# Pairs of sequences as units of the sample group's sparse attention, with scores on eight TensorE tiles of 64 rows and 32 columns

## The chip, the cores and the metric

The kernel is one launch on one core of a Trainium2 chip. The metric is the device time of the launch in microseconds (us), as the median of several runs. Four compute engines matter here: TensorE (PE, matmuls and transposes), VectorE (DVE), ScalarE (ACT) and GpSimd (POOL); SyncE's queue (SP) issues the page loads. TensorE writes its results into PSUM, which is handed out in banks of 128 partitions by 512 floats.

## The reference, cut to what matters

Two token groups go through a two-layer decoder trunk: a prompt of 512 tokens, and a sample group of 8 sequences with 8 new tokens each and 4096 past tokens. The change lies in layer 1's sparse attention of the sample group. For every query head it has three branches: compressed keys (255 of them), the past's 64 blocks of 64 keys of which a top-16 choice is kept by a mask, and a window of 512 keys; the new tokens' own 8 keys are added to the last two.

```
s_c = where(ok_c, einsum('btghd,bngd->btghn', qf, kc), NEG);  p_c = softmax(s_c);  o_c = p_c @ vc
imp = einsum('btghn,ns->btgs', p_c, m_ov);  top_v, top_i = top_k(imp, 16)
s_s = where(ok_s, qf . k_sel, NEG);  p_s = softmax(s_s);  o_s = p_s @ v_sel
s_w = where(ok_w, qf . k_win, NEG);  p_w = softmax(s_w);  o_w = p_w @ v_win
return gates[0] * o_c + gates[1] * o_s + gates[2] * o_w
```

A sequence has 16 heads in 4 groups of 4; a group shares its keys and values, and a head is 64 wide. So for one sequence and one group there are 32 query rows (4 heads by 8 tokens), and the scores of a group contract over 64 elements.

## The kernel before

The trunk runs in stages: layer 0, its feed-forward with the compression of the past's pages beside it, the projections of layer 1's attention, the attention itself, the output projection, memory attention and the last feed-forward. The attention stage is the one that matters here. In it two Python generators are woven: `prompt_attend` (40 steps of the prompt's attention, `one`) and `sample_attend` (`other`). The weaving is the loop at the end of `mixer_nsa`: after prompt step `i` it takes sample units until their count is 1.76 (i + 1). The sample generator has 76 units: 4 of compressed scores (two sequences each), 8 windows (one sequence each), and 64 selected units (one sequence, one chunk of 512 past keys). The instructions are then ordered for each engine by a scheduler that works with priorities and modelled times, so what stands next to what on an engine is not in the source; each engine works its own list in order. `together` asks that a group of matmuls follow their first.

One selected unit loads a "page" tile of 1 MB (`pg`, four transfers of 256 KB by `load_pages`, L1106: keys in the first half of a row, values in the second), and then:

- two score matmuls (L1622) into one PSUM bank `ss_ps`. The page's keys lie with one key group in partitions 0 to 63 and the next in 64 to 127; the queries `qz` are stored with zeros in the half that is not theirs, so that each matmul contracts over all 128 rows and gives 64 columns of the array (two groups by 32 rows). The two matmuls write partitions 0 to 63 and 64 to 127.
- the mask, the scale and the row's maximum on DVE (`scores`, L1480), which empties the bank, and the exponential with its sum on ACT (`expo`, L1483);
- four transposes (L1492) into `st_ps`, a copy to `spT` on ACT or DVE in turn (L1494), and 16 matmuls of 32 columns (L1499) into `oa_ps`, a bank that collects all 8 chunks of a sequence.

After a sequence's eighth chunk, L1631 to L1644 weigh the chunks and add them to `orow`; at the end of all, `or_ps` (L1662) transposes `orow` into `oT`, which the output projection reads. The scores of the prompt (`sc_ps`), the compressed keys (`cs_ps`), the windows (`sw_ps`) and the new keys (`sn_ps`) share three PSUM banks (tag "sc") with `ss_ps`; transposes and small outputs share three more (tag "tp"). Pages have five buffers at first; whenever ten prompt steps are done, the queries of a prompt group are no longer needed and give one buffer more (`pgq`).

Of the kernel before, what the change touches and what calls it, by code (L numbers as in the profile page):

```python
# [83 lines left out]
_nv("nmask", 512)  # L84
# [8 lines left out]
def _nsa_constants():  # L93
# [11 lines left out]
    bb, t = j // 64, p % TS  # L105
    kb, kt = (j % 64) // TS, j % TS
    put("nmask", np.where((bb == kb)[None, :] & (kt[None, :] <= t[:, None]), 0, NEG))
# [54 lines left out]
def tile_step(ctx: ExitStack, tc: tile.TileContext, I, O):  # L162
# [949 lines left out]
    gD = dp.tile([48, TS, NB], F32, name="gD")  # L1112
# [4 lines left out]
    def mixer_nsa():  # L1117
        with ExitStack() as c0:
# [12 lines left out]

            kp = c0.enter_context(pool(name="nkeep", bufs=1))
            qz = kp.tile([P, NB, 2, 64], F32, name="qz")
            G.memset(qz, 0.0)
            ksn = kp.tile([P, 2, 2, 64], F32, name="ksn")
            vsn = kp.tile([64, 512], F32, name="vsn")
            sgate = kp.tile([P, 3, NB], F32, name="sgate")
# [34 lines left out]
            with ExitStack() as c1:  # L1172
# [81 lines left out]
    def nsa_queries(ch, xh, xl, rc, wk, pst, ax, qH, qz):  # L1254
        if True:
            ps = proj_tm(pst, I["w_in1t"][2 + ch], xh, xl, TOKS)
            for i, t0, n, kt in head_rows(ps, rc, wk, late["nrow"][:, 0:64], lambda i: wk.tile([P, 512], F32, tag="kt", name="qt", bufs=5)):
# [12 lines left out]
                else:  # L1270
# [4 lines left out]
                    for e in range(2):  # L1275
                        for b in range(NB):
                            V.tensor_copy(qz[e * 64 : (e + 1) * 64, b, ch, e * 32 : (e + 1) * 32].rearrange("p (h t) -> p h t", h=4),
                                          tp[e * 64 : (e + 1) * 64, 4 * e : 4 * e + 4, b * TS : (b + 1) * TS])

    def nsa_gates(xh, xl, rb, wk, pst, ax, gT, sgate):  # L1280
# [6 lines left out]
        sgt = wk.tile([48, TS, NB], F32, tag="cpg", name="sgt", bufs=1)  # L1287
        V.tensor_scalar_add(sgt, sg[:, TP:].rearrange("p (b t) -> p t b", t=TS), 1.0)
        V.reciprocal(sgt, sgt)
        nc.scalar.dma_start(gD, sgt)  # L1290
        for r in range(3):
            nc.scalar.dma_start(sgate[:, r, :], gD.rearrange("(h r) t b -> r h t b", r=3)[r])
# [71 lines left out]
    def prompt_compressed(N, wk, pa, qH, kc2, gT, pcT):  # L1364
# [21 lines left out]
        for tt, (sc, mx) in enumerate(rows):  # L1386
            V.tensor_reduce(mx, sc, axis=AX.X, op=ALU.add)
            V.reciprocal(mx, mx)
            V.tensor_mul(mx, mx, gT[:, tt, 0::3])
# [8 lines left out]
    def prompt_attend(N, wk, pa, po, qH, ktm, vsb, gT, pcT, vcz, oT):  # L1398
# [3 lines left out]
        for g in range(4):  # L1402
# [11 lines left out]
            for pr in range(2):  # L1414
# [3 lines left out]
                for pieces in (((0, 3),), ((0, 0), (0, 2)), ((0, 1), (1, 1)), ((1, 0), (1, 2)), ((1, 3),)):  # L1418
# [23 lines left out]
                    for i, (br, tt, q) in enumerate(at):  # L1442
                        r = 3 * (4 * g + h0) + 1 + br
                        V.tensor_mul(sm[:, i, :], sm[:, i, :], gT[:, tt, r : r + 4 : 3])
# [29 lines left out]
    def sample_attend(N, wk, page, pa, po, qz, ksn, vsn, sgate, orow, mrow, oT):  # L1474

        def scores(ps, mask, s, mn):
# [6 lines left out]
        def output(o, s, v, first, last, flip, behind=None):  # L1485

            tp = pa.tile([P, 4, P], F32, tag="tp", name="st_ps")
            pT = wk.tile([P, 4, P], F32, tag="spT", name="spT")
            lead = None
            for i in range(4):  # L1490
                with together(lead):
                    mm = TE.transpose(tp[:, i, :], s[:, i * P : (i + 1) * P], ident)  # L1492
                lead = lead or mm.ins
            (S.copy if flip else V.tensor_copy)(pT, tp)  # L1494
            lead = None
            for i in range(4):
                for g in range(4):
                    with together(lead) if lead is not None or behind is None else tc.issue_after(behind):
                        mm = TE.matmul(o[g * 32 : (g + 1) * 32, :], pT[:, i, g * 32 : (g + 1) * 32], v[:, i, g * 64 : (g + 1) * 64],  # L1499
                                       start=first and i == 0, stop=last and i == 3)  # L1500
                    lead = lead or mm.ins
            return mm.ins

        def output_new(o, br, s, first):
# [4 lines left out]
            for g in range(4):  # L1509
                TE.matmul(o[g * 32 : (g + 1) * 32, :], pT[:, g * 32 : (g + 1) * 32], vsn[:, br * 256 + g * 64 : br * 256 + (g + 1) * 64],  # L1510
# [7 lines left out]
        def compressed(b0):  # L1518

            kv = page().rearrange("p (b e i f) -> p b e i f", b=2, e=2, i=2)  # L1520
            for b in range(2):
                nc.sync.dma_start(kv[:, b, 0], kcD[b0 + b])
                nc.sync.dma_start(kv[:, b, 1], vcD[b0 + b])
            ps = pa.tile([P, 2, 256], F32, tag="sc", name="cs_ps")
            for b in range(2):
                for gp in range(2):
                    TE.matmul(ps[gp * 64 : (gp + 1) * 64, b, :], qz[:, b0 + b, gp, :], kv[:, b, 0, gp, :], start=True, stop=True)
            mx = wk.tile([P, 2], F32, tag="cmx", name="cmx")
            V.tensor_reduce(mx, ps[:, :, :255], axis=AX.X, op=ALU.max)
            V.tensor_scalar_mul(mx, mx, -0.125)  # L1530
            p = wk.tile([P, 2, 256], F32, tag="ss", name="cp", bufs=3)
            sm = wk.tile([P, 2], F32, tag="csm", name="csm")
            V.memset(p[:, :, 255:], 0.0)
            for b in range(2):
                S.activation(p[:, b, :255], ps[:, b, :255], AF.Exp, bias=mx[:, b : b + 1], scale=0.125, accum_out=sm[:, b : b + 1])
# [3 lines left out]
            for b in range(2):  # L1539
                for i in range(2):  # L1540
                    TE.transpose(tp[:, b, i, :], p[:, b, i * P : (i + 1) * P], ident)
# [3 lines left out]
            for b in range(2):  # L1545
                for i in range(2):
                    for g in range(4):
                        TE.matmul(oc[g * 32 : (g + 1) * 32, b, :], pT[:, b, i, g * 32 : (g + 1) * 32], kv[:, b, 1, i, g * 64 : (g + 1) * 64],
                                  start=i == 0, stop=i == 1)
            V.tensor_mul(orow[:, b0 : b0 + 2, :], oc, sgate[:, 0, b0 : b0 + 2].unsqueeze(2).to_broadcast([P, 2, 64]))  # L1550
# [5 lines left out]
            q0 = (b0 % 4) * 32  # L1556
            for b in range(2):
# [302 lines left out]
```

## Time and profile before

| what | value |
|---|---|
| time, median of 3 runs (lowest to highest) | 2393.67 us (2391.99 to 2395.39) |
| profiled execution: its time, its span | 2394.9 us, 2393.1 us |
| TensorE busy, share of the span | 2335.8 us, 98% |
| attention stage, about | from 1450 to 1795 us |
| in it, busy: PE, DVE, ACT | 328.4, 263.8, 200.1 us of 345 |

Matmuls are shown with partitions contracted by columns of the array ("128\*64"). A float32 matmul leaves two records, a transpose one. The records of a run of matmuls overlap, so what a run takes is read from its start to the start of the next run, not from the length of a record. The profiled execution lies 1.2 us above the median.

### The profile page before, as it was taken

How to read it: one execution, taken by the hardware profiler on the slowest of the kernel's cores; microseconds unless marked ns; L12 is line 12 of the kernel's file. 1: busy time of each engine (PE TensorE's matmuls, PEld its weight loads, DVE VectorE, ACT ScalarE, POOL GpSimd, SP SyncE). 2: the span in 40 equal slices, each digit the busy share in tenths (PEclk: the TensorE clock that was granted, in tenths of full speed). 3: DMA queues.
4: the chain of work that ended last, by engine and by line, in shares of the span. 5: the costliest groups of instructions: out<-in, count | busy, mean ns of one | idle time of the engine just before them, and what ended most of it. 6: DMA issues, size and time to landing. Idle time of an engine off the chain costs nothing. (4 is left out here: it accounts for less than half of the span.)

```text
span 2393.1 us, 51279 instructions
## 1 busy us (share of the span) xinstructions
PE 2335.8 (98%) x19363; PEld 2118.5 (89%) x19363; DVE 1490.1 (62%) x3357; ACT 1007.3 (42%) x1940; POOL 468.0 (20%) x579
## 2 busy tenths in 40 slices
PE   8999999998999999999999998999999899999999
PEld 8999889986999999999998875566669699999999
DVE  7766564676767777775435867787776774333333
ACT  4333123354555555553224545565564452122221
POOL 2146453121112122213011420000002111010100
PEclk9999999999999999999999999999999999999999
DMA  4221332245366776673421226678872422424222
GB/s 159 80 66 36 132 124 81 76 150 194 112 206 206 212 226 212 201 228 101 135 71 40 87 70 227 215 242 266 265 263 95 166 89 76 161 73 158 72 94 84
DMA packets 181833, 344.25 MB, mean 144 GB/s; under 512 B 21073, under 2 KB 93394, under 8 KB 180050
## 3 DMA queue, kind: packets, MB, share of 16 engines
q1 hardware_dynamic: 173106, 315.75, 41.2%
q10 hardware_dynamic: 8480, 25.23, 2.8%
q8 instruction: 153, 2.51, 0.4%
q14 instruction: 94, 0.77, 0.1%
HBM read 319.44 MB, written 25.47 MB: 144 GB/s over the span
## 5 line engine op out<-in xcount | busy, mean ns | idle before, releaser
L213 ACT CAST whi<-raw 128x1024 fp32r<-128x1024 f32 (+4 forms) x278 | 258.7, 931 | 672.2 <-PE pj L240 568.1
L215 DVE TENSOR_TENSOR wlo<-raw,whi 128x1024 fp32r<-128x1024 f32 (+4 forms) x278 | 317.1, 1141 | 66.5 <-ACT whi L213 58.8
L240 PE MATMUL pj<-fxl,whi 128*128 128x256 f32 (+1 forms) x1408 | 306.8, 296 | 0.0
L240 PE MATMUL pj<-fxh,whi 128*128 128x256 f32 (+1 forms) x1408 | 306.7, 297 | 0.0
L240 PE MATMUL pj<-fxh,wlo 128*128 128x256 f32 (+1 forms) x1408 | 306.2, 296 | 0.0
L1067 DVE TENSOR_TENSOR clo<-craw,chi 128x512 fp32r<-128x512 f32 x256 | 201.6, 802 | 92.2 <-ACT chi L1066 84.1
L240 PEld LDWEIGHTS pj<-fxl,whi 128*128 128x128 f32 x1408 | 237.9, 190 | 0.0
L240 PEld LDWEIGHTS pj<-fxh,wlo 128*128 128x128 f32 x1408 | 237.7, 190 | 0.0
L240 PEld LDWEIGHTS pj<-fxh,whi 128*128 128x128 f32 x1408 | 237.6, 190 | 0.0
L1066 ACT CAST chi<-craw 128x512 fp32r<-128x512 f32 x256 | 155.4, 620 | 117.0 <-PE c_ps L1077 101.0
L967 POOL TENSOR_TENSOR fg<-fg,rb 128x576 f32<-128x576 f32 x44 | 75.7, 1720 | 504.3 <-ACT fg L966 504.1
L240 PE MATMUL pj<-xl,whi 128*128 128x256 f32 (+1 forms) x768 | 171.2, 301 | 0.0
L240 PE MATMUL pj<-xh,wlo 128*128 128x256 f32 (+1 forms) x768 | 169.4, 300 | 0.0
L240 PE MATMUL pj<-xh,whi 128*128 128x256 f32 (+1 forms) x768 | 169.3, 300 | 0.0
L240 PE MATMUL pj<-al,whi 128*128 128x256 f32 x704 | 154.4, 296 | 0.0
L240 PE MATMUL pj<-ah,whi 128*128 128x256 f32 x704 | 154.4, 296 | 0.0
L240 PE MATMUL pj<-ah,wlo 128*128 128x256 f32 x704 | 153.6, 296 | 0.0
L1075 PE MATMUL c_ps<-chi,w1h 128*128 128x256 f32 (+1 forms) x512 | 143.5, 283 | 2.5 <-ACT chi L1066 2.5
L1076 PE MATMUL c_ps<-clo,w1h 128*128 128x256 f32 (+1 forms) x512 | 144.6, 284 | 0.5 <-DVE clo L1067 0.4
L1077 PE MATMUL c_ps<-chi,w1l 128*128 128x256 f32 (+1 forms) x512 | 144.4, 284 | 0.0
L240 PEld LDWEIGHTS pj<-xl,whi 128*128 128x128 f32 x768 | 129.8, 190 | 4.7 <-issue 4.0
L240 PEld LDWEIGHTS pj<-xh,wlo 128*128 128x128 f32 x768 | 129.8, 190 | 2.4 <-issue 1.7
(544 smaller groups left out, 5244.3 us busy)
## 6 DMA issues: line engine op xcount, KB each, us to landing
craw<-in_cmpP SPq DMA_DIRECT2D x512, 128.0 KB, 3.0
pg<-in_slcP SPq DMA_DIRECT2D x192, 256.0 KB, 3.9
raw<-in_w_in SPq DMA_DIRECT2D x48, 512.0 KB, 3.5
raw<-in_w_gate SPq DMA_DIRECT2D x44, 512.0 KB, 3.4
raw<-in_w_up SPq DMA_DIRECT2D x44, 512.0 KB, 3.2
pgq<-in_slcP SPq DMA_DIRECT2D x64, 256.0 KB, 3.9
raw<-in_w_down SPq DMA_DIRECT2D x32, 384.0 KB, 3.7
raw<-in_w_down SPq DMA_DIRECT2D x32, 320.0 KB, 2.9
```

Of the source, the lines that this page charges most:

```text
L213: S.copy(hi, raw)
L215: V.tensor_sub(lo, raw, hi)
L240: TE.matmul(ps[h], w[:, k, :], x[k0 + k][:, t0:t1], start=f and first, stop=e and last)
L967: G.tensor_mul(t, t, rb)
L1066: S.copy(hx, rv)
L1067: V.tensor_sub(lx, rv, hx)
L1075: TE.matmul(ps[:, :n], w1h[:, kv, jj, :], hv, start=jj == 0, stop=False)
L1076: TE.matmul(ps[:, :n], w1h[:, kv, jj, :], lv, start=False, stop=False)
L1077: TE.matmul(ps[:, :n], w1l[:, kv, jj, :], hv, start=False, stop=jj == 7)
```

## The change

The sample's unit becomes a pair of sequences (`pr`, sequences 2 pr and 2 pr + 1), with 40 units in all: 4 compressed, 4 windows and 32 selected. `qz` loses its zeros and is half as wide. The scores of a pair are eight matmuls (`products`), each over 64 rows of the array and 32 of its columns: the row half `x` is the half of the partitions in which the key group lies, the column place is given by group pair and sequence. The four with `x` = 1 fill one bank, the four with `x` = 0 another. Transposes and outputs are then also done for both banks at a time (8 transposes, 32 output matmuls); one bank is copied by ACT and one by DVE. `oa_ps` holds four chunks of a pair instead of eight of a sequence, so after the fourth chunk ACT copies it away. The weaving takes 0.93 units a prompt step. The order of the gates, masks and `orow` follows the new rows; the gates come through two stores and one load.

```diff
-                    while n < 1.76 * (i + 1):
+                    while n < 0.93 * (i + 1):
...
+        SLOTS = [(gp, b) for gp in range(2) for b in range(2)]
+        def products(ps, pr, keys):
+            first = None
+            for b in (1, 0):
+                for x in (1, 0):
+                    for gp in range(2):
+                        i = 2 * gp + b
+                        h = slice(x * 64, (x + 1) * 64)
+                        with together(first):
+                            mm = TE.matmul(ps[x][i * 32 : (i + 1) * 32], qz[h, 2 * pr + b, gp, :], keys(b, gp)[h], start=True, stop=True)
+                        first = first or mm.ins
...
+        def turned(s):
+            tp = [pa.tile([P, 4, P], F32, tag="tp", name="st_ps") for _ in range(2)]
+            pT = [wk.tile([P, 4, P], F32, tag="spT", name="spT") for _ in range(2)]
...
+            S.copy(pT[0], tp[0])
+            V.tensor_copy(pT[1], tp[1])
...
+        def selected(pr):
...
-                pg = page().rearrange("p (k f) -> p k f", k=4)
-                load_pages(b, 4 * c, 4, [lambda k: pg[:, k, :]], I["slcP"])
-                ps = pa.tile([P, 4, P], F32, tag="sc", name="ss_ps")
-                for gp in range(2):
-                    TE.matmul(ps[gp * 64 : (gp + 1) * 64, :, :], qz[:, b, gp, :], pg[:, :, gp * P : (gp + 1) * P], start=True, stop=True)
-                s = wk.tile([P, 512], F32, tag="ss", name="ss", bufs=3)
...
+                pg = []
+                for b in range(2):
+                    p = page().rearrange("p (k f) -> p k f", k=4)
+                    load_pages(2 * pr + b, 4 * c, 4, [lambda k, p=p: p[:, k, :]], I["slcP"])
+                    pg.append(p)
+                ps = [pa.tile([P, 4, P], F32, tag="sc", name="ss_ps") for _ in range(2)]
+                products(ps, pr, lambda b, gp: pg[b][:, :, gp * P : (gp + 1) * P])
+                s = [wk.tile([P, 512], F32, tag="ss", name="ss", bufs=4) for _ in range(2)]
+                for x in range(2):
+                    scores(ps[x].rearrange("p i (k x) -> p (i k) x", k=2),
+                           mrow[:, 2 * pr + x, c * 8 : (c + 1) * 8].unsqueeze(2).to_broadcast([P, 8, 64]),
+                           s[x].rearrange("p (k x) -> p k x", k=8), mn[:, x, c : c + 1])
+                    expo(s[x], mn[:, x, c : c + 1], sm[:, x, c : c + 1])
+                pT = turned(s)
+                if c % 4 == 0:
+                    oa = po.tile([P, 2, 4, 64], F32, tag="oa", name="oa_ps")
+                last = output(lambda x: oa[:, x, c % 4, :], pT, lambda b: pg[b][:, :, 256:], True, last)
+                if c == 3:
+                    S.copy(t, oa)
...
+            for src, dst, c0 in ((t, o1, 0), (oa, o2, 4)):
+                u = wk.tile([P, 2, 4, 64], F32, tag="ss", name="su", bufs=4)
+                for x in range(2):
+                    V.tensor_mul(u[:, x], src[:, x], f[:, x, c0 : c0 + 4].unsqueeze(2).to_broadcast([P, 4, 64]))
+                    V.tensor_reduce(dst[:, x, :], u[:, x].rearrange("p c d -> p d c"), axis=AX.X, op=ALU.add)
```

On TensorE, where the prompt turns to its second group of heads, a selected unit's two score matmuls stand in the kernel before as one row (`sc_ps` and `kt_ps` are the prompt's scores and key transposes):

```order
L1430 MATMUL sc_ps<-kHH,qH 128x512 x2
L1622 MATMUL ss_ps<-pg,qz 64x512 x2
L1430 MATMUL sc_ps<-kLL,qH 128x512 x2
L1412 MATMUL kt_ps<-cst,kd 128x128 x4
L1622 MATMUL ss_ps<-pg,qz 64x512 x2
```

In the changed kernel the eight of a pair stand there in two halves of four, the first four being those with `x` = 1 (one bank), the last four those with `x` = 0:

```order
L1433 MATMUL sc_ps<-kHH,qH 128x512 x2
L1464 MATMUL o_ps<-pcT,vcz 64x512 x2
L1492 MATMUL ss_ps<-pg,qz 32x512 x2
L1492 MATMUL ss_ps<-pgq,qz 32x512 x2
L1433 MATMUL sc_ps<-kLL,qH 128x512 x2
L1415 MATMUL kt_ps<-cst,kd 128x128 x4
L1492 MATMUL ss_ps<-pg,qz 32x512 x2
L1492 MATMUL ss_ps<-pgq,qz 32x512 x2
```

What moved: the prompt's second score matmuls and its key transposes now lie between the two halves of one unit's scores. Over the list, 21 of the 32 selected units stand in two halves like this one, with other tile shapes between them, and 11 stand as one run of eight; of those 11, five have a wait for DVE on the first matmul of the second bank, after four of the first.

On TensorE at the end of the stage, the last units stand before as follows, one sequence each (`st_ps` are the transposes, `oa_ps` the outputs):

```order
L1492 MATMUL st_ps<-cst,ss 128x128 x8
L1622 MATMUL ss_ps<-pg,qz 64x512 x2
L1467 MATMUL o_ps<-PT,vsb 64x128 x8
L1492 MATMUL st_ps<-cst,ss 128x128 x4
L1499 MATMUL oa_ps<-pgq,spT 32x64 x32
L1492 MATMUL st_ps<-cst,ss 128x128 x8
L1622 MATMUL ss_ps<-pg,qz 64x512 x2
L1499 MATMUL oa_ps<-pg,spT 32x64 x32
```

In the changed kernel the last two pairs stand there with their scores whole:

```order
L1509 MATMUL st_ps<-cst,ss 128x128 x8
L1457 MATMUL pt_ps<-cst,S 128x128 x4
L1492 MATMUL ss_ps<-pg,qz 32x512 x8
L1457 MATMUL pt_ps<-cst,S 128x128 x4
L1523 MATMUL oa_ps<-pgq,spT 32x64 x32
L1509 MATMUL st_ps<-cst,ss 128x128 x8
L1470 MATMUL o_ps<-PT,vsb 64x128 x8
L1492 MATMUL ss_ps<-pg,qz 32x512 x8
```

What moved: transposes and outputs always come in runs of 8 and 32, and the last unit is a whole pair. From the first `cs_ps` to the last `or_ps`, TensorE's list changes its tile shape 329 times before and 308 times in the changed kernel; `oa_ps` stands in 50 runs before and in 32 now.

## Rows read from the trace of the kernel before

**Rows 1.** The stage in stretches; columns stand in the first line.

```profile
core 0: us, PE busy (x) PEld busy (x) DVE busy (x) ACT busy (x) POOL busy (x), PEclk, DMA share, GB/s
1450.00:1513.00 63.00, 56.89 (x711) 36.26 (x711) 48.67 (x207) 33.37 (x103) 1.36 (x4) 0.97 0.66 231
...
1560.00:1765.00 205.00, 202.47 (x2885) 133.20 (x2883) 161.89 (x574) 122.64 (x354) 1.84 (x3) 1.00 0.80 260
1765.00:1795.00 30.00, 24.66 (x440) 18.21 (x439) 20.87 (x44) 16.37 (x32) 0.00 (x0) 0.89 0.71 245
sum 345.00, PE 328.40 PEld 216.71 DVE 263.76 ACT 200.13 POOL 4.43; mean PE 82.10 PEld 54.18 DVE 65.94 ACT 50.03 POOL 1.11
```

**Rows 2.** Timeline of TensorE, 1652 to 1671 us: start, length, what.

```profile
1653.80 1.08 PE L1622 MATMUL ss_ps<-pg,qz 128*64 128x512 f32 x4
1654.81 0.50 PE L1430 MATMUL sc_ps<-kHH,qH 128*128 128x512 f32 x1
...
1656.95 1.10 PE L1499 MATMUL oa_ps<-pg,spT 128*32 128x64 f32 x64
1657.98 1.09 PE L1454 MATMUL pt_ps<-cst,S 128*128 128x128 f32 x8
1658.91 0.60 PE L1492 MATMUL st_ps<-cst,ss 128*128 128x128 f32 x4
...
1663.47 0.65 PE L1499 MATMUL oa_ps<-pg,spT 128*32 128x64 f32 x32
1664.06 0.30 PE L1506 MATMUL stn_ps<-cst,sn 128*64 128x128 f32 x1
```

**Rows 3.** Instructions on the tile `ss_ps`: ns min/median/max, first and last start.

```profile
L1622 PE MATMUL ss_ps<-pg,qz x192: 592/592/644, 1513.8 to 1778.3; 128*64 128x512 f32 x192
L1480 DVE CUSTOM_DVE_ANT_1 ss<-ss_ps,mrow x64: 659/686/693, 1514.9 to 1779.0; 128x512 f32<-128x512 f32 x64
```

**Rows 4.** Instructions on the tile `ow_ps`.

```profile
L1510 PE MATMUL ow_ps<-vsn,spn x64: 216/228/241, 1480.5 to 1529.3; 64*32 64x64 f32 x64
```

**Rows 5.** Timeline of all engines, 1640 to 1650 us.

```profile
1642.45 0.68 DVE L1480 CUSTOM_DVE_ANT_1 ss<-ss_ps,mrow 128x512 f32<-128x512 f32 x1
...
1643.06 0.09 DVE L1480 DVE_READ_ACCUMULATOR2_ANT smn<- 128x1 f32 x1
...
1643.34 0.72 ACT L1483 ACTIVATE ss<-ss,smn 128x512 f32<-128x512 f32 x1
```

**Rows 6.** Who waited for whom, 1450 to 1795 us: total, times, longest.

```profile
PEld sc_ps L1430 <- DVE sm L1444: 5.3, 7, 0.8
PEld ss_ps L1622 <- DVE mn L1438: 4.6, 9, 0.7
...
PE ss_ps L1622 <- DMA pg<-in_slcP: 1.6, 4, 0.5
```

**Rows 7.** The chain that ended last, 1600 to 1615 us.

```profile
1605.01 0.63 PE oa_ps L1499 x32
...
1606.72 1.66 SPq L1106
...
1608.55 2.96 DMA pg<-in_slcP
...
1611.65 1.08 PE ss_ps L1622 x4
```

**Rows 8.** The page's part on DMA issues: count, size, us to landing.

```profile
pg<-in_slcP SPq DMA_DIRECT2D x192, 256.0 KB, 3.9
```

**Rows 9.** Timeline of all engines, 1755 to 1800 us: the end of the stage.

```profile
1777.80 1.08 PE L1622 MATMUL ss_ps<-pg,qz 128*64 128x512 f32 x4
...
1782.89 1.04 PE L1662 MATMUL or_ps<-cst,orow 128*64 128x64 f32 x28
...
1785.54 0.69 DVE L1640 TENSOR_TENSOR st<-oa_ps,sf 128x512 f32<-128x512 f32 x1
...
1786.26 1.01 DVE L1642 TENSOR_REDUCE so<-st 128x64 f32<-128x512 f32 x1
1787.31 0.28 DVE L1643 SCALAR_TENSOR_TENSOR so<-osn,sf,so 128x64 f32<-128x64 f32 x1
...
1787.91 0.34 PE L1662 MATMUL or_ps<-cst,orow 128*64 128x64 f32 x4 [2.95 <-DVE orow L1644]
```

More of the change, by code (lines that the diff above doesn't have):

```diff
@@ L83 @@
 _nv("cmask", 512)
-_nv("nmask", 512)
+_nv("nmask", 256)
 _nv("wmask", 512)
@@ L1483, in expo, with output, output_new @@
             S.activation(s, s, AF.Exp, bias=mn, scale=-1.0, accum_out=sm)
[L1485 to L1501, printed above, removed]
+        def turned(s):
+            tp = [pa.tile([P, 4, P], F32, tag="tp", name="st_ps") for _ in range(2)]
+            pT = [wk.tile([P, 4, P], F32, tag="spT", name="spT") for _ in range(2)]
+            first = None
+            for x in (1, 0):
+                for i in range(4):
+                    with together(first):
+                        mm = TE.transpose(tp[x][:, i, :], s[x][:, i * P : (i + 1) * P], ident)
+                    first = first or mm.ins
+            S.copy(pT[0], tp[0])
+            V.tensor_copy(pT[1], tp[1])
+            return pT
+        def output(o, pT, v, last, behind=None):
+            first = None
+            for x in (1, 0):
+                for i in range(4):
+                    for k, (gp, b) in enumerate(SLOTS):
+                        g = 2 * gp + x
+                        with together(first) if first is not None or behind is None else tc.issue_after(behind):
+                            mm = TE.matmul(o(x)[k * 32 : (k + 1) * 32, :], pT[x][:, i, k * 32 : (k + 1) * 32],
+                                           v(b)[:, i, g * 64 : (g + 1) * 64], start=i == 0, stop=last and i == 3)
+                        first = first or mm.ins
             return mm.ins
-        def output_new(o, br, s, first):
+        def output_new(o, br, x, s, first):
             tp = pa.tile([64, P], F32, tag="tp", name="stn_ps")
@@ new lines, in selected @@
+        def selected(pr):
+            mn = wk.tile([P, 2, 9], F32, tag="smn", name="smn")
+            sm = wk.tile([P, 2, 9], F32, tag="ssm", name="ssm")
+            sn = new_scores(pr, 0, lambda x: mn[:, x, 8:9])
+            on = pa.tile([P, 2, 64], F32, tag="tp", name="on_ps")
+            for x in range(2):
+                expo(sn[x], mn[:, x, 8:9], sm[:, x, 8:9])
+                output_new(on[:, x, :], 0, x, sn[x], True)
+            osn = wk.tile([P, 2, 64], F32, tag="osn", name="osn")
@@ L1645, in selected @@
+            for x in range(2):
+                V.scalar_tensor_tensor(o1[:, x, :], osn[:, x, :], f[:, x, 8:9], o1[:, x, :], op0=ALU.mult, op1=ALU.add)
+            V.tensor_add(o1, o1, o2)
+            o = orow[:, 2 * pr : 2 * pr + 2, :]
+            V.tensor_add(o, o, o1)
             yield
         for f in range(2):
-            compressed(4 * f)
-            yield
-            compressed(4 * f + 2)
-            yield
+            for pr in (2 * f, 2 * f + 1):
+                compressed(pr)
+                yield
@@ L1652, in sample_attend @@
             choose(f)
-            for b in range(4 * f, 4 * f + 4):
-                window(b)
+            for pr in (2 * f, 2 * f + 1):
+                window(pr)
                 yield
-        for b in range(NB):
-            yield from selected(b)
+        for pr in range(4):
+            yield from selected(pr)
         tp = pa.tile([P, NB, 8, TS], F32, tag="tp", name="or_ps")
-        for b in range(NB):
-            for e in range(2):
-                TE.matmul(tp[e * 64 : (e + 1) * 64, b, :, :], orow[:, b, :],
-                          ident.rearrange("p (k e t) -> p k e t", e=2, t=TS)[:, :, e, :], start=True, stop=True)
+        for pr in range(4):
+            for x in range(2):
+                for e in range(2):
+                    for b in range(2):
+                        TE.matmul(tp[e * 64 : (e + 1) * 64, 2 * pr + b].rearrange("p (g x k) t -> p x g k t", g=2, x=2)[:, x],
+                                  orow[:, 2 * pr + x, :],
+                                  ident.rearrange("p (g b k e t) -> p b e g k t", g=2, b=2, e=2, t=TS)[:, b, e], start=True, stop=True)
```

174 lines of the change are left out of this document (83 added, 91 removed).

## The prediction, made before the changed kernel was run

> **What bounds the kernel now.** I read the stretches of the attention stage first [rows 1]. TensorE is busy 328.4 of 345 us, VectorE 263.8 and ScalarE 200.1; from 1560 to 1765 us TensorE is busy 202.47 of 205 us and the granted clock is 1.00, the upper of its two levels (2.4 GHz). So the stage ends when TensorE's list ends, and a saving counts if it shortens that list and no wait takes its place. The reserves are small: the DMA engines are busy 0.80 of that stretch at 260 GB/s, and VectorE 162 of 205 us.
>
> The timeline of TensorE [rows 2] gives the price of each kind of run, from its start to the start of the next. One unit's two score matmuls take 1654.81 - 1653.80 = 1.01 us. A single unit's 32 output records take 1664.06 - 1663.47 = 0.59, and two units' 64 in one run take 1657.98 - 1656.95 = 1.03. Two single runs would be 1.18, so a change of tile shape costs about 0.15 and 32 records 0.44. Without its shape change the score run is 0.86, that is two passes of 0.43: each float32 matmul has two records [rows 3], and the two matmuls, which lie in different column halves of the array, run side by side, or it would be four passes. Eight transposes take 1658.91 - 1657.98 = 0.93.
>
> **The change, part by part.**
>
> *Selected scores.* Before: 64 units x 0.86 = 55.0 us. Now a pair has eight matmuls of 32 columns and 64 rows. Four of them (one row half) fill all 128 columns and cost two passes, 0.86. If the two row halves also run side by side, the eight cost 0.86 as well, half of the old price for two sequences. But that only happens where all eight stand together on TensorE. In the order of the changed kernel 21 of the 32 units stand in halves with other tile shapes between; these cost 2 x 0.86 = 1.72, as before. Six are whole: 0.86. Five are whole but wait for VectorE to give back a bank after the first four: between 0.86 (the wait is over when it comes) and 1.72; I take the middle, 1.29, since the wait's price hangs on where VectorE stands. Sum: 21 x 1.72 + 6 x 0.86 + 5 x 1.29 = 36.1 + 5.2 + 6.5 = 47.8, that is **-7.2** (-9.4 to -5.1).
>
> That row halves run side by side isn't shown by any row of before. The nearest row has 64 rows by 32 columns too, but all its tiles lie in one row half [rows 4], at a median of 228 ns a record. From below the gain is 0: the halves one behind the other, 1.72 for every unit. I take the full overlap, because tiles that share no column already overlap completely in [rows 2], and the tiles here share no bank either: x = 0 and x = 1 write different ones. The Trainium skill states the same, in "TensorEngine Tiling (Array Packing)", Key Properties: tiles operate independently, and different tiles can load weights and multiply in parallel. By it a whole unit would be 0.86; no row of before shows it for row halves.
>
> *Windows and compressed scores.* By the same count: windows 8 x 0.86 = 6.9 become 3 x 1.72 + 0.86 + ~0.5 of waiting = 6.5; compressed 8 x 0.43 = 3.4 become 2 x 0.86 + 2 x 0.43 = 2.6, or 3.0 with a wait. **-0.8** (-1.2 to 0).
>
> *Shape changes.* 329 become 308: 21 x 0.15 = **-3.2** (-3.2 to 0, if a change of row count is dearer than the 0.15 measured between shapes of 128 rows).
>
> *Joining `orow`.* 16 matmuls become 32 (shapes of 64 columns, 32 records' pitch 0.44 at most): 0 to +1.0, taken **+0.5**.
>
> *The tail.* The last unit ends the stage. Before, from its scores at 1777.80 to the last `or_ps` at 1787.91 lie 10.1 us [rows 9]. Now, its scores being two banks, VectorE works through a second one (0.69, and 0.09 to read the maximum back [rows 5]) = +0.76; four more transposes 0.46 (half of the 0.93); 16 more output matmuls (32 records) 0.44. Finishing goes in four pieces of half the size: 0.69 + 1.01 + 0.28 in [rows 9] become the same elements in two and two more starts, +0.6 estimated from two more of the 0.28 of the smallest piece. Together **+2.3** (+1 to +4). All other units' additional latency lies under the prompt's work on TensorE.
>
> *Both pages before the scores.* A pair's scores stand behind two pages. A page is four transfers of 256 KB, 3.9 us from issue to landing [rows 8]; 1 MB at 260 GB/s [rows 1] is 4.0 us, so a pair waits that much longer for its second page, where nothing was loaded ahead. Before, TensorE lost 1.6 us to pages in the stage [rows 6]. 0 to +4; taken **+0.5**, since buffers increase from five to eight and hold pages ahead.
>
> *Less cover for VectorE and ScalarE.* What they do in the stage stays nearly the same in sum: a pair has two banks to mask, exponentiate and copy, as two units had. TensorE already waits 5.3 and 4.6 us for them [rows 6]; the same work for them beside a shorter list leaves more. 0 to +11 (all of the gain); taken **+1.5**, because VectorE has 345 - 264 = 81 us free in the stage, though bound to moments.
>
> *What lies outside.* The memset of `qz` falls away and a few small operations before the stage swap places under a TensorE that is busy without a gap: 0, +/-2 us for their order.
>
> Sum: -7.2 - 0.8 - 3.2 + 0.5 + 2.3 + 0.5 + 1.5 = -6.4. From the profiled execution's 2394.9 us that is 2388.5; it lies 1.2 us above the median, so I say **2387 us** against 2393.67.
>
> **The rivals.**
>
> A. *The gain in full.* All eleven whole units cost 0.86 and no new wait comes up: -9.4 - 1.2 - 3.2 + 0.5 + 2.3 = -11.0, **2383 us**. For it: 81 us of VectorE's time are free. Against it: the five units whose second half carries a wait.
>
> B. *The banks take over.* One bank costs VectorE 0.69 + 0.09 us and ScalarE another 0.72 for the exponential [rows 5]; a pair now asks for two of three banks at one time, and the prompt, whose scores share them, waits behind. TensorE's list shortens, and its waits grow by as much: the -11.0 become about 0 plus the tail, **2394 us**, +/-3. For it: TensorE's longest entries in the table of waits are for VectorE already [rows 6], on just these tiles. Against it: none is longer than 0.8 us. The Trainium skill has this as a rule, in "TensorEngine Tiling (Array Packing)", PSUM Bottleneck: tiling speeds up the multiplications, not the emptying of PSUM, which may become the bottleneck.
>
> C. *The row halves don't run side by side.* Then the change doesn't do what it says: scores 0, shape changes -3.2, joining, tail, pages and waits +4.8: +1.6, **2395 us**. For it: no row of before shows the overlap. Against it: the argument from column tiles.
>
> D. *Slower: pages in pairs.* A page's buffer is occupied from its load to the end of its outputs. In [rows 2] from the scores at 1653.80 to the end of the outputs at 1664.06 it lives 10.3 us. In the chain [rows 7] a released buffer (1605.01 + 0.63) has its next scores at 1611.65, 6.0 us later, and for a pair 4.0 more: 10.0. So two buffers are occupied 20.3 us per pair. Sixty-four pages in the 277 us from 1513 to 1790 need a pair every 8.6 us. With six buffers (three pairs) that holds up to a life of 3 x 8.6 - 10.0 = 15.8 us. That is the point from which it decides: with a life of 20 us a pair comes every 10.0 us, 1.4 too late, and over the some ten pairs until the seventh buffer comes that is +14: **2401 us**. For it: the halves of 21 units stand apart, which lengthens the life; the DMA share is 0.80 already. Against it: 10.3 us now, and TensorE's waits for pages are only 1.6 us.
>
> **How the numbers follow.** The forecast has 0.35, A 0.20, B 0.20, C 0.07, D 0.18. What a measurement of this kernel can tell from no change is about 0.2%, 4.8 us: faster means under 2388.9, slower over 2398.5. The forecast with its own range of 2380 to 2391 (the bounds of scores, shape changes and tail) lies about 0.27 in faster and 0.08 in same; A is faster; B is 0.03 faster, 0.15 same, 0.02 slower; C is 0.05 same and 0.02 slower; D, whose price may be small, is 0.02 faster, 0.03 same and 0.13 slower. Together faster 0.52, same 0.31, slower 0.17. The range, 2376 to 2400 us, reaches from A with seven of the split units overlapping after all (7 x 0.86 = 6.0 more) to a D with a life of some 19 us, and leaves out about 0.2.
>
> **What would show it.** In the profile of the changed kernel: whole runs of eight score matmuls should take about 1.0 us from start to start, and split ones 1.0 for each half; if whole ones take 1.9, C is right. TensorE's busy time in the stage should fall from 328 by about 10 us, its idle time rise by 3 to 5. If the idle time rises by 10 behind VectorE or ScalarE on `ss_ps` and `sc_ps`, it is B; if SP's queue or the page transfers end the waits before `ss_ps`, it is D. The time from the last `ss_ps` to the last `or_ps` should be about 12.4 us instead of 10.1. The prediction would be wrong above all if the row halves overlapped with what stands between them, so that split units gained too, or if the price of a shape change were other between row counts.

## The result and the profile after

| kernel | median us (lowest to highest) | ratio to before, 95% interval |
|---|---|---|
| before | 2393.15 (2391.99 to 2395.39) | |
| changed | 2427.63 (2421.29 to 2428.06) | 1.0130 (1.0114 to 1.0146) |

The change made the kernel 34 us slower. The profiled execution has a span of 2425.6 us. The windows view of the stage stands against [rows 1]; the stage now ends at 1822 us, and the columns are the same:

```profile
core 0: us, PE busy (x) PEld busy (x) DVE busy (x) ACT busy (x) POOL busy (x), PEclk, DMA share, GB/s
1450.00:1513.00 63.00, 54.99 (x748) 35.39 (x748) 52.43 (x220) 37.03 (x113) 2.31 (x5) 0.97 0.64 220
1513.00:1560.00 47.00, 40.80 (x598) 26.96 (x594) 26.30 (x98) 18.13 (x52) 1.23 (x2) 0.85 0.62 195
1560.00:1765.00 205.00, 185.64 (x2826) 120.12 (x2818) 144.34 (x513) 110.66 (x320) 1.84 (x3) 0.98 0.73 232
...
1795.00:1825.00 30.00, 20.46 (x435) 16.57 (x432) 18.14 (x43) 13.57 (x28) 0.00 (x0) 0.88 0.67 227
```

Two columns have moved. From 1560 to 1765 us TensorE is busy 185.6 instead of 202.5 us, and the granted clock is below 1.00 in four of the five stretches (0.85 from 1513 to 1560 us, where it had been 1.00), so part of the work was done at the lower level of 1.2 GHz. VectorE and ScalarE do no more than before in the whole stage (260 and 195 us, before 260 and 196), and the DMA engines move less per second, not more. So nothing became busier: TensorE waits. For what, the table of waits says, for TensorE from 1450 to 1825 us (total, times, longest):

```profile
PE ss_ps L1492 <- DMA pg<-in_slcP: 15.2, 10, 2.6
PE ss_ps L1492 <- DMA pgq<-in_slcP: 5.3, 2, 3.5
PE or_ps L1709 <- DVE orow L1690: 4.3, 1, 4.3
```

20.5 us for pages. Before, [rows 6] has 1.6 for `pg`, and the same table has for `pgq`:

```profile
PE ss_ps L1622 <- DMA pgq<-in_slcP: 1.2, 2, 0.7
```

The timeline of SP's queue and of TensorE around one such wait shows how it comes about:

```profile
1559.92 1.89 SPq L1107 DMA_DIRECT2D pg<-in_slcP  x4
...
1572.40 0.22 PE L1523 MATMUL oa_ps<-pg,spT 128*32 128x64 f32 x1
...
1572.66 2.24 SPq L1107 DMA_DIRECT2D pgq<-in_slcP  x4
1576.55 5.54 SPq L1107 DMA_DIRECT2D pg<-in_slcP  x8
...
1582.54 0.63 PE L1492 MATMUL ss_ps<-pg,qz 64*32 64x512 f32 x3 [1.09 <-DMA pg<-in_slcP]
```

SP issues nothing from 1561.81 to 1572.66 us: no buffer is free until an older pair's last output ends at 1572.62. Then the pair's first page is issued at once, its second only at 1576.55 (the table entries are read in between), and the scores start at 1582.54, 9.9 us after the release. That is rival D's turn of 10.0 us. Four stops of 9.4 to 10.9 us stand between page loads in the stage; before, the three longest are 5.5 to 7.2 us.

For the account of the stage I take it from its first `pct_ps` to the first matmul of the output projection. TensorE's busy time and its idle time are those of the windows; "work" is the busy time less half of what lay at the lower clock level by the clock's record, so an estimate of what the list would take at 2.4 GHz. The rows below "changed" belong to the experiments.

| profiled execution of | stage us | busy | at the lower level | work | idle | of it ahead of `ss_ps` |
|---|---|---|---|---|---|---|
| before | 341.8 | 324.5 | 3.4 | 322.8 | 17.3 | 4.4 |
| changed | 369.7 | 329.1 | 29.7 | 314.4 | 40.6 | 22.3 |
| changed, run again | 370.5 | 324.7 | 20.5 | 314.4 | 45.8 | 25.8 |
| pairs, old scores | 364.2 | 325.3 | 21.7 | 314.4 | 38.9 | 22.7 |
| half loads: before | 335.9 | 322.9 | 6.2 | 319.8 | 13.0 | 1.1 |
| half loads: pairs, old scores | 329.9 | 316.6 | 6.7 | 313.3 | 13.3 | 0.0 |
| half loads: changed | 338.2 | 318.1 | 6.7 | 314.8 | 20.1 | 1.6 |
| half loads, two-bank tiles: old scores | 353.9 | 323.5 | 17.9 | 314.6 | 30.4 | 2.3 |
| half loads, two-bank tiles: eight tiles | 341.0 | 299.6 | 24.3 | 287.5 | 41.3 | 3.0 |
| six buffers: changed | 354.6 | 323.4 | 21.3 | 312.8 | 31.2 | 9.9 |
| six buffers: pairs, old scores | 351.0 | 318.2 | 12.7 | 311.8 | 32.7 | 7.3 |

So +27.9 us in the stage are +23.3 of idle time, +13.2 of clock (half of 29.7 less half of 3.4) and -8.4 of work, within rounding. The remaining 4.7 us of the profiled difference lie ahead of the stage. They aren't put down to the change: the stage starts between 1443.5 and 1453.5 us in the profiled executions of all kernels here, and the changed kernel run again starts it 5.0 us earlier than the first time. The clock fell behind some of the waits: TensorE stood idle for 3.5 us up to 1636.3, and from 1636.6 us on its clock is at the lower level. But 9.4 us of the 29.7 lie between 1520.5 and 1530.7 us, ahead of the first selected scores; what TensorE had waited for just ahead of them was VectorE, three times for 0.4 to 0.6 us, and no page. The changed kernel run again has 20.5 us at the lower level, so the clock's part is 8.6 to 13.2 us.

### The profile page after: what moved, and what is told of

It reads as the page before. It is cut to its first block, busy times and chain, and to the rows that moved or that the text cites. A ratio compares the mean times of both kernels' runs of the same rounds, so it can differ in the third digit from the quotient of the medians.

```text
span 2425.6 us, 52092 instructions
## 1 busy us (share of the span) xinstructions
PE 2343.5 (97%) x19779; PEld 2123.9 (88%) x19779; DVE 1493.2 (62%) x3361; ACT 1005.9 (41%) x1936; POOL 465.4 (19%) x578
## 4 chain that ended last, share of the span: by engine, by line
PE 81%; DVE 7%; DMA 4%; SPq 3%; issue 2%; ACT 2%; POOL 0%; ACTq 0%; DVEq 0%; POOLq 0%
PE pj L241 52%; SPq L1107 2%; PE c_ps L1077 2%; PE c_ps L1078 2%; PE c_ps L1076 2%; DMA pg<-in_slcP 2%; PE ss_ps L1492 2%; PE tm_ps L253 1%; PE tm_ps L254 1%; PE tm_ps L252 1%; PE sc_ps L1433 1%; PE o_ps L1470 1%; DMA craw<-in_cmpP 1%; DVE wlo L216 1%; PE pt_ps L1457 1%
## 5 line engine op out<-in xcount | busy, mean ns | idle before, releaser
L1068 DVE TENSOR_TENSOR clo<-craw,chi 128x512 fp32r<-128x512 f32 x256 | 206.6, 821 | 92.3 <-ACT chi L1067 76.8
```

The costliest lines, as they stand in the source:

```text
L1068: V.tensor_sub(lx, rv, hx)
```

## The experiments

Ratios are to the kernel before, run beside each on the same chip.

**Pairs alone, old scores.** The kernel before with the selected units as pairs; its windows and compressed scores stay single, and it is woven at 1.76 units a step, a pair counting two. Against the changed kernel, the selected scores differ in this line:

```diff
-                        mm = TE.matmul(ps[x][i * 32 : (i + 1) * 32], qz[h, 2 * pr + b, gp, :], keys(b, gp)[h], ...)
+                        mm = TE.matmul(ps[b][gp * 64 : (gp + 1) * 64, :, :], qz[:, 2 * pr + b, gp, :], pg[b][:, :, gp * P : (gp + 1) * P], ...)
```

> The kernel before with one part of the change alone: selected units are pairs of sequences with two pages each, but each sequence's scores are the old two matmuls over 128 rows and 64 columns (one bank per sequence). The diagonal mask of the new keys is kept in a shorter table, which frees the space for a fourth score tile. Theory 1 (a pair holds two page buffers until its outputs and gets both back only then, so TensorE waits for pages): it is as slow as the changed kernel or a little slower, 2425 to 2445 us, with 15 to 30 us of TensorE idle ahead of ss_ps. Theory 2 (the eight tiles themselves: row halves that don't overlap, or banks that VectorE gives back late): without the tiles the loss is gone, 2388 to 2400 us.

2411.98 us, ratio 1.0054 (1.0033 to 1.0075). It lies between the two ranges: the pairs alone cost 19 us. Its waits are those of the changed kernel, here from 1450 to 1825 us:

```profile
PE ss_ps L1628 <- DMA pg<-in_slcP: 15.7, 13, 2.8
PE or_ps L1702 <- DVE orow L1683: 3.9, 1, 3.9
PE ss_ps L1628 <- DMA pgq<-in_slcP: 3.8, 2, 2.9
```

19.5 us for pages without any eight-tile product. And TensorE's work in the stage is 314.4 us, as in the changed kernel.

**Both pages' table entries first.**

```diff
+                rg = [page_indices(2 * pr + b, 4 * c, 4) for b in range(2)]
-                    load_pages(2 * pr + b, 4 * c, 4, [lambda k, p=p: p[:, k, :]], I["slcP"])
+                    load_pages(2 * pr + b, 4 * c, 4, [lambda k, p=p: p[:, k, :]], I["slcP"], rg[b])
```

> The changed kernel, but SP reads the table entries of both pages of a pair before it issues the first page's transfers, so that the second page is issued right behind the first. Theory 1 (pages): a pair's turn gets about 1.4 us shorter of some 26; with three pairs in rotation that is 0.5 us per pair and, over 28 pairs, 8 to 20 us with the clock that comes back: 2407 to 2420 us. Theory 2 (tiles, banks): no change, 2422 to 2430 us.

2428.77 us, 1.0133 (1.0106 to 1.0160): no gain, as the theory of the tiles had it; the expectation for pages failed. From a pair's last issue to its first score the median over the 32 pairs is 5.9 us, and was 4.8; from its first issue to its scores it is 10.3 instead of 10.7. So the 1.4 us were hardly won: what the second issue gained, the wait behind it gave back. That the two pages' 2 MB, now in one burst, take longer to land is the likely reason, not shown.

**Half of the loads left out**, in the changed kernel, in the kernel before, and in the pairs with old scores. In the pairs both sequences use one page, as below; in the kernel before every second chunk of a sequence uses the page of the chunk ahead of it.

```diff
-                for b in range(2):
+                for b in range(1):
                     p = page().rearrange("p (k f) -> p k f", k=4)
...
-                    pg.append(p)
+                    pg += [p, p]
```

> The changed kernel with half of the selected loads left out: both sequences of a pair use the first one's page (keys and values of the second sequence are not those of the reference). Theory 1 (pages): the waits ahead of ss_ps (22 us) go, and most of the half-clock time that follows them (some 10 us): 2378 to 2392 us; TensorE idle in the stage falls from 40 to under 20 us. Theory 2 (tiles, banks): stays above 2412 us.

> The kernel before with half of the selected loads left out in the same way (each page serves two chunks; keys and values of every second chunk are not those of the reference). It is the yardstick for the changed kernel with half of the loads: the difference of the two is what eight tiles and pairs give when pages cost nothing. Theory 1: before hardly waits for pages, so 2386 to 2393 us, and the changed kernel with half loads lies 5 to 12 us below it. Theory 2: the changed kernel lies well above it.

> Pairs of sequences with the old scores, with half of the selected loads left out (both sequences use the first one's page, so the second's keys and values are not those of the reference). It stands between the two half-load runs: before 2386.5, changed 2393.3 us. If the eight tiles cost nothing of their own and only gain (7 us by the forecast), it lies at 2395 to 2402 us; if they cost more than they gain, at 2380 to 2390 us.

Changed: 2393.26 us, 0.9994 (0.9979 to 1.0010), just above the range of the theory of pages. Before: 2386.49, 0.9959 (0.9940 to 0.9977). Pairs with old scores: 2385.05, 0.9956 (0.9930 to 0.9982). By the medians leaving out half of the loads gives back 7 us to the single units, 27 to the pairs and 34 to the changed kernel; by the ratios, which take each chip's own runs of before, 10, 23 and 33. So pages cost pairs with the old scores 14 to 20 us more than single units, and the changed kernel 23 to 27 more. With half of the loads, pairs as such cost nothing. But the changed kernel, which was to gain by its eight tiles, costs 8 to 9 us more than they do even then, for 6.8 us more idle time and 1.5 more work. The theory that pages are everything was wrong in this.

Where this idle time lies can be read from the two traces. Up to the end of the last window's output (`ow_ps`) TensorE stands idle for 10.6 us in the changed kernel and for 7.5 in the pairs with old scores, from there to the last selected scores for 3.1 and 0.3, behind them for 6.4 and 5.6. So less than half of the 6.8 us lies in the stretch that holds nearly all selected scores (30 of 32 pairs); 3.1 lies ahead of it, where windows and compressed scores run as pairs, too, and the weaving differs.

**The changed kernel again, and units of one page with eight tiles** of 256 keys:

```diff
-            for c in range(8):
+            for c in range(16):
+                pg = page().rearrange("p (b k f) -> p b k f", b=2, k=2)
+                for b in range(2):
+                    load_pages(2 * pr + b, 2 * c, 2, [lambda k, b=b: pg[:, b, k, :]], I["slcP"])
```

> The changed kernel once more, unedited, as the yardstick for the three that run beside it: 2420 to 2430 us by every theory. After the first four runs two causes stand: pages (a pair turns two buffers over together) and the clock that falls after each wait. A rival is left: that pairs alone cost 19 us, and the eight tiles cost the remaining 15 by something of their own.

> The changed kernel with units of one page: a pair of sequences with 256 past keys each in one buffer of 1 MB (two transfers of each sequence), scores still in eight tiles of 64 rows and 32 columns, but 256 keys wide; 16 chunks to a pair, four transposes in one bank and 16 outputs to a chunk. The weaving takes 1.66 units a prompt step, so that as much work is left behind the prompt. The pages' cause: the waits ahead of ss_ps fall to the 4 us of before, and the time to 2385 to 2398 us; VectorE has twice as many, half as long score operations, some 0.1 us more a chunk, 6 to 10 us in sum, hidden. Eight tiles as the cause: it stays above 2408 us.

> The version with one page a unit once more, woven by work: its pairs of windows now count two units (before, eight units that are worth twelve were taken at the pace of single ones, and the stage's first 60 us had the most idle time and the clock at 0.90). If this was why it lost, 2390 to 2412 us. If the smaller units' score banks are the cause (each half-size unit takes two of the three banks, and TensorE waited 20 us for VectorE ahead of ss_ps and sc_ps), it stays at 2420 to 2435 us.

Changed again: 2430.73 us, 1.0161 (1.0127 to 1.0195). One page: 2432.40, 1.0158 (1.0130 to 1.0185); woven by work 2437.83, 1.0196 (1.0164 to 1.0227). The expectations for pages failed. The first lies where it put the eight tiles as the cause (above 2408 us), the second 3 us above the higher of its two ranges. The tile `ss_ps` of the first one and its waits:

```profile
L1497 DVE CUSTOM_DVE_ANT_1 ss<-ss_ps,mrow x128: 393/419/431, 1520.3 to 1810.0; 128x256 f32<-128x256 f32 x128
```

```profile
PE ss_ps L1492 <- DMA pg<-in_slcP: 9.2, 4, 2.5
PE ss_ps L1492 <- DVE smn L1497: 5.6, 3, 3.1
...
PE sc_ps L1433 <- DVE smn L1497: 3.4, 2, 3.2
```

Half the columns take VectorE 0.42 us instead of 0.69, so it is busy 278.6 us in the stage (260.4 in the changed kernel), ScalarE 218.7 (194.8). Each small unit takes two banks until VectorE is through, and TensorE waits 9.0 us for it in the lines above. The waits for pages fell to 9.2 us, not to 4, and TensorE's idle time in the stage is 43.5 us, with 50.1 us of its work at the lower clock level (40.6 and 29.7 in the changed kernel). Since the edit changed VectorE's part as well as the pages', it decides nothing between pages and tiles.

**Weaving by work.** The changed kernel counts a pair as one unit and so starts the pages later.

```diff
-                    while n < 0.93 * (i + 1):
+                    while n < 1.76 * (i + 1):
...
                     yield
+                    yield
```

> The changed kernel, woven by work as before: each pair of windows or selected pages counts two units and the pace is 1.76 again, so that the first selected pair comes as early as the first selected unit did (the changed kernel's 0.93 a step counts the four compressed units like the rest and starts the pages some 19 us later, at 1532 instead of 1514 us). If the late start is part of the loss, 2405 to 2422 us; if only the pairs' turn over of pages and the eight tiles count, 2424 to 2434 us as the changed kernel.

2429.72 us, 1.0142 (1.0118 to 1.0166): no change beyond the intervals. The later start doesn't explain the loss.

**A sixth page buffer.** The room comes from the same cuts in both kernels of the first pair.

```diff
-                        s = wk.tile([P, 512], F32, tag="S", name="S", bufs=4)
+                        s = wk.tile([P, 512], F32, tag="S", name="S", bufs=3)
...
-            gp_ = pk.enter_context(pool(name="npg", bufs=5, side="right"))
+            gp_ = pk.enter_context(pool(name="npg", bufs=6, side="right"))
```

> The changed kernel with some tiles' buffers cut (S and PT of the prompt from 4 to 3, ss from 4 to 3, sn from 4 to 2, osn to 1, so2 laid into st), which frees the room for one more page, but still with five page buffers. It only serves as the yardstick of the next: 2425 to 2450 us, as the cuts take cover away.

> The same cuts with six page buffers at first, nine at the end. Pages' cause: with one more buffer of six a pair's turn of 26 us is shared by half a pair more, so 10 to 25 us less than with five, and the waits ahead of ss_ps fall by a third or more. Eight tiles as the cause: no change against five, within 4 us.

> The changed kernel with the cuts and six page buffers, woven by work as in the run beside it. If buffers and weaving add up, 2395 to 2408 us; if the six buffers already made up for the late start, as with six alone, 2408 to 2416 us.

Five: 2421.28 us, 1.0113 (1.0086 to 1.0140). Six: 2412.38, 1.0080 (1.0054 to 1.0107); woven by work 2408.56, 1.0073 (1.0045 to 1.0102). The cuts alone were expected to cost; with five buffers they lie 9 us below the changed kernel run beside them. The sixth buffer gives 9 us more, a little less than expected, and the waits of TensorE for pages fall from 14.8 us with five (11.0 and 3.8) to

```profile
PE ss_ps L1492 <- DMA pg<-in_slcP: 4.7, 2, 2.8
PE ss_ps L1492 <- DMA pgq<-in_slcP: 3.0, 3, 1.3
```

**Pairs with old scores and six buffers, and single units with five and six.** The room comes from much the same cuts.

> Pairs with the old scores, with cuts and six page buffers: beside the changed kernel with cuts and six buffers (2412 us) it shows what the eight tiles in halves cost when pages bind less. If they cost as much as with half of the loads (8 us) or with all (16 us), 2394 to 2406 us; if the cost came with the pages alone, 2408 to 2414 us.

> The yardstick of the kernel before with six page buffers (2389 us against 2396): the same cuts in tiles' buffers, but still five page buffers. Its list on TensorE changes shape 302 times from the first compressed score to the last joining of outputs, against 296 with six and 328 in the kernel before, because cut buffers let less stand between. If the sixth buffer made the gain, 2392 to 2398 us; if the shorter list did, 2387 to 2391 us.

> The kernel before, one sequence to a unit, with six page buffers instead of five (room from S and PT with three buffers instead of four, a shorter table for the new keys' mask, and single buffers of small tiles). With half of its loads it gained 7 us, so pages cost it at most that: 2387 to 2396 us; the pairs' gain from the sixth buffer was 9 us.

Pairs with old scores: 2400.16 us, 1.0028 (1.0015 to 1.0040), 12 us below the changed kernel with six buffers. Single units with five: 2391.82, 0.9999 (0.9987 to 1.0012); with six: 2388.90, 0.9973 (0.9964 to 0.9983). The last is faster than both kernels, and the cuts alone don't do it: the sixth buffer gives the single units 3 us.

**Scores whole.** Tiles of two banks, of which there are two, let all eight matmuls of a pair become possible at once; the rest gets two banks. With half of the loads, with eight tiles and with old scores, and once with all loads and six buffers.

```diff
-                ps = [pa.tile([P, 4, P], F32, tag="sc", name="ss_ps") for _ in range(2)]
+                ps = pa.tile([P, 2, 512], F32, tag="sc", bufs=2, name="ss_ps")
+                ps = [ps[:, x, :].rearrange("p (i k) -> p i k", i=4) for x in range(2)]
```

> The changed kernel with half of the selected loads left out as before (the second sequence of a pair uses the first one's keys and values), and scores in tiles of two PSUM banks each, of which there are two (four banks; transposes and small outputs get two instead of three). So all eight score matmuls of a pair become possible at the same moment, and on TensorE's list 32 of 32 units stand whole. The windows' outputs for the new keys get a place of their own and are added by VectorE, as two banks less allow no second output tile. If eight tiles side by side gain what the forecast says of a whole unit (0.86 us), TensorE's work in the stage falls by some 20 us against the run beside it, and the time by 5 to 20 us, as waits for VectorE take some of it: 2370 to 2385 us. If tiles cost something of their own even when whole, it is no faster than the run beside it.

> The yardstick of the run beside it: pairs with the old scores (128 rows by 64 columns), half of the loads left out in the same way, the same two tiles of two banks for scores and two banks for the rest. Against the same kernel with three and three banks (2385 us) the two banks for transposes cost something: 2385 to 2400 us.

> The changed kernel complete, with all loads, with the cuts and six page buffers and scores in two tiles of two banks, so that the eight stand whole. Beside six buffers alone (2412 us) it shows whether whole units help while pages bind: if TensorE's list is what ends the stage, 2390 to 2402 us; if pages still end it, 2405 to 2414 us, with longer waits for pages instead of work.

Eight tiles: 2396.43 us, 1.0007 (0.9994 to 1.0020). Old scores: 2407.89, 1.0057 (1.0040 to 1.0073). All loads: 2418.85, 1.0105 (1.0081 to 1.0128). All three lie above their ranges. The timeline of TensorE in the first:

```profile
1698.82 1.09 PE L1493 MATMUL ss_ps<-pg,qz 64*32 64x512 f32 x16
1699.84 0.50 PE L1434 MATMUL sc_ps<-kLL,qH 128*128 128x512 f32 x1
```

A pair's eight matmuls take 1.02 us with their shape change, and TensorE's work in the stage falls by 314.6 - 287.5 = 27.1 us. To see how much of it the selected scores give, I add up what TensorE spends on a tile: from the start of each of its runs to the start of the next run, less idle time and less half of what lay at the lower clock level. By this the selected scores fall from 59.1 to 35.7 us, by 23.4, where 32 x 0.86 = 27.5 was to be expected; the windows', the compressed and the new keys' scores give another 8.2, and other tiles take 4 more. So where they stand whole the tiles gain what their price says, and the time is 11.5 us below that of old scores. But idle time rises by 10.9, and with two banks for transposes and outputs the old scores lie 23 us above their kin with three, the eight tiles 3 us (within the intervals). With all loads pages still end the waits ahead of `ss_ps`: 18.8 us of them, and 40.7 us of busy time at the lower clock level.

## Why the prediction was wrong

The forecast was 2387 us, the time 2427.6; the sign was wrong. By its own steps:

- *Selected scores*: the price of a run held. Lines of the changed kernel's timeline of TensorE show a whole unit, one that waited for a bank, and a half, each with the line behind it:

```profile
1532.35 1.09 PE L1492 MATMUL ss_ps<-pg,qz 64*32 64x512 f32 x16
1533.37 0.50 PE L1433 MATMUL sc_ps<-kHH,qH 128*128 128x512 f32 x1
...
1559.72 2.00 PE L1492 MATMUL ss_ps<-pg,qz 64*32 64x512 f32 x16
1561.66 1.09 PE L1457 MATMUL pt_ps<-cst,S 128*128 128x128 f32 x8
...
1688.14 1.06 PE L1492 MATMUL ss_ps<-pg,qz 64*32 64x512 f32 x8
1689.14 1.09 PE L1457 MATMUL pt_ps<-cst,S 128*128 128x128 f32 x8
```

  Whole: 1.02 us from start to start; in the changed kernel this is the only whole unit that had neither a wait just ahead of it nor one inside, but with half of the loads and two-bank tiles 23 of 32 took it. So the row halves do run side by side, and rival C is out. That agrees with the rule of the Trainium skill, "TensorEngine Tiling (Array Packing)", Key Properties, that tiles work in parallel. With a wait for the second bank: 1.94, the upper bound; of the five such units three cost that, two some 1.23, so the middle of 1.29 (1.44 with a shape change) was too low. Halves: 0.99 each in most units. By the count of the two-bank tiles TensorE spent 59.5 us on the selected scores, after 64.2 before: 4.7 less, for 7.2 forecast. Pairs with old scores have the same 314.4 us of work in the stage: beside them the selected scores took 3.1 us less, but the prompt's scores (`sc_ps`) 2.6 and its outputs (`o_ps`) 1.6 more. The longer runs of outputs (`oa_ps`) and transposes (`st_ps`), which both have, took 2.8 and 1.6 less than before.
- *Shape changes, joining*: 10.7 us less work had been forecast from these steps and the scores together, 8.4 came. That size is no cause of the loss.
- *The tail*: from the last scores at 1805.98 to the last `or_ps` at 1820.23 it is 14.3 us, for a forecast of 12.4 (at most 14.1). In the chain that ended last it reads:

```profile
1801.37 4.48 DMA pg<-in_slcP
...
1805.98 1.45 PE ss_ps L1492 x16
...
1812.79 0.76 DVE su L1684 x2
...
1815.32 1.22 DVE wlo L216
1816.55 0.19 DVE so L1687
1816.74 1.14 DVE wlo L216
...
1820.23 0.70 PE or_ps L1709 x16
```

  Two operations on the next stage's weights (`wlo`) stand among the pieces in which VectorE finishes the last pair; before, the chain has one of 1.13 us there. The forecast had no term for the second.
- *Both pages before the scores*: this step failed. I took +0.5 (0 to +4); idle time ahead of `ss_ps` rose by 22.3 - 4.4 = 17.9 us, and TensorE's waits for pages from 2.8 to 20.5. I had priced how much later a second page lands, and taken buffers as ahead of the scores; I had not asked how often a pair finds no buffer free. Before, a page's scores came 7.7 us after its last issue (median of 64), so it lay there when it was wanted; now 4.8 (median of 32), which is hardly more than its landing takes (4.1).
- *Rival D* named this cause and its side, at 0.18. Its threshold, a life of 15.8 us, was compared with 10.3 us of one unit in [rows 2]. Over all 64 units the median life, from the first score to the last output, is 13.5 (7.2 to 18.6); in the changed kernel it is 16.6, past the threshold. Its price was too small as well: one fixed rate stood for a queue that stops 10 us at a time.
- *The clock* had no term: +13.2 us, or 8.6 in the changed kernel run again. Some of it follows the waits for pages; 9.4 us of the work at the lower level in the first run lie ahead of all selected scores.
- *Less cover*: +1.5 taken (0 to +11). The idle time not ahead of `ss_ps` rose by 23.3 - 17.9 = 5.4, inside the range.
- *Rival B* alone didn't happen, but it waits behind the pages: with half of the loads and whole units 27.1 us less work gave 11.5 us of time, with 10.9 us more idle time, most of it ahead of `sc_ps`, `o_ps`, `pt_ps` and `on_ps`, whose banks VectorE and ScalarE empty. This agrees with the Trainium skill, "TensorEngine Tiling (Array Packing)", PSUM Bottleneck: tiling doesn't speed up the emptying of PSUM.

In sum, the greater part of the 34 us is pages turned over in pairs. This is shown, by ways that agree: pairs with old scores have the waits and 19 us of the loss without any eight-tile product; half of the loads takes the waits away, and with them 14 to 20 us more from these pairs than from single units, 23 to 27 more from the changed kernel; and a sixth buffer gives 9 us to the changed kernel, 3 to the single units. Since the two kernels of pairs lose different amounts to pages, the parts don't simply add.

The rest comes with what the changed kernel has beyond pairs with old scores: eight tiles, mostly in halves, for selected scores, windows and compressed scores, and the slower weaving, whose undoing changed nothing. By the medians it is 8 us with half of the loads, 12 with six buffers and 16 with five and all loads. In the profiled executions the stage shows 8.3, 3.6 and 5.5 of it, so only the first is seen there as a whole. Which part makes it isn't shown. The halves of the selected scores, with other shapes and waits for banks between, can be one part, but in the half loads much of the additional idle time lies beside the windows. No run joined the halves and kept everything else, since the two-bank tiles cost transposes and outputs a bank, and none kept the windows single beside the eight tiles. This stays open.

## What to carry to other kernels

When units are merged, count buffers first: the life of a buffer from load to release, over all units and not one, times the buffers that a unit takes at once, against the rate at which units are wanted. A gain by side-by-side tiles exists only where the order sets them side by side, and the order is known before the run; here 21 of 32 units stood in halves of 0.99 us each, and three of the others paid 1.94 us for the bank they waited for. One more page buffer for the old single units, with the cuts that made room, gave a little where the change lost: 0.9973 (0.9964 to 0.9983).

## What was not expected of the hardware

Row halves overlap fully, which was forecast without a row that showed it: eight matmuls of 64 rows by 32 columns took 1.02 us, as long as the four of one half with their shape change (0.99). Reading the table entries earlier brought a pair's scores only 0.4 us nearer to its first issue (10.3 us instead of 10.7). And idle time in pieces of one to four us came with a loss through the clock: 13.2 us beside 23.3 us more idle time in one execution of the changed kernel, 8.6 beside 28.5 in another.
